# First pair of heads: the second head's loads move to GpSimd, its query cast is split, and one of its transposes moves ahead of the second group

## The chip, the core and the metric

The kernel runs on one core of a Trainium2 chip. The metric is the device time of one execution in microseconds (us). The kernel before took 118.14 us, the median of three runs (117.71, 118.14 and 118.82).

## The reference

Attention over 8 batches and 8 heads of 512 positions and 64 dimensions, in float32, softmax over the keys:

```python
scale = 1.0 / np.sqrt(q.shape[-1])
scores = np.einsum('bhqd,bhkd->bhqk', q, k) * scale
scores = scores - scores.max(axis=-1, keepdims=True)
attn = np.exp(scores)
attn = attn / attn.sum(axis=-1, keepdims=True)
return np.einsum('bhqk,bhkd->bhqd', attn, v).astype(np.float32)
```

## The kernel before

The 64 heads are worked on as 32 pairs. A head has four blocks of 128 queries and four blocks of 128 keys. Q, K and V of a pair are loaded as float32, cast to float16, and Q and K are transposed on TensorE so that the 64 dimensions lie on the partitions. Scores are made transposed: one matmul gives a block of 128 keys on the partitions against all 512 queries, from 64 rows. Two such blocks, one on the upper and one on the lower 64 rows of the array, make a "group", a PSUM tile of 128 x 1024, and one exponential turns it into float16 probabilities in SBUF (line 594; line 780 for the first three groups). Line 683 multiplies the probabilities with V, which carries a column of ones, so that the sums of the softmax come with the result; VectorE inverts and scales (lines 655 and 663), and SyncE stores. Twelve of the groups are exponentiated by VectorE with a polynomial instead (lines 612 and 634), four of these with help from GpSimd (lines 647 and 650). All else of the exponentials is ScalarE's.

The order of the instructions is fixed by hand (`tc.manual_schedule()`). A planner, the class `Plan`, walks through a model of the engines once and gives a list of steps, which are then issued in that order on each engine's queue. It starts behind the first pair of heads with constants, and nothing of it depends on how the first pair is done. Each engine runs its own queue in order, and a wait holds whatever is behind it on that engine.

Ahead of the planner's steps stands the opening, in this order of the source:

- `first_loads` (line 723): Q and K of the first pair, one load of 128 KB for each head. The keys go through ScalarE's queue (line 727), the queries through SyncE's (line 728).
- The loads of the next pairs, 256 KB each, on SyncE's queue (line 498).
- `make_identity`: GpSimd writes `ident`, the identity that every transpose needs. Then VectorE's memsets of `lift` and of the column of ones in V.
- `first_pair` (line 734). Casts to float16: `q16` holds each query block twice side by side, so that a transpose puts it on both the upper and the lower 64 rows. Head 0's casts are spread over VectorE (lines 746, 747), ScalarE (748) and GpSimd (749). Head 1's keys are cast by ScalarE (750), its queries by GpSimd in one instruction (751).
- TensorE, meanwhile, runs `busy` matmuls on a constant (line 732), whose results nobody reads. They are called fillers here. Behind them come head 0's transposes: two blocks of queries, the keys in two pieces, two more blocks of queries, three fillers. VectorE copies the results out of PSUM into `qt` and `kt` (lines 794 to 797).
- The first groups. Group 0 is done in two halves of 256 queries, `st_0a` and `st_0b`, each with an exponential of its own; group 1 is `st1`. Then head 1's four query transposes into `pqb` and two key transposes into `pkb` (lines 808 to 813), VectorE's copies of them (810, 814), four fillers, and group 2, `st2`, with the fourth exponential (line 818). Group 3 is the first of the planner's (line 589), followed by the transposes of pair 1 (line 544) and VectorE's copies of them (line 551).

In this text the scores of `st_0a`, `st_0b`, `st1` and `st2` are called first, second, third and last scores, and the exponentials of line 780 first to fourth.

Of the kernel before, what the change touches and what calls it, by code (L numbers as in the profile page):

```python
# [404 lines left out]
def kernel(  # L405
# [7 lines left out]
    nc = tc.nc  # L413
    B, H, S, D = q.shape
    P = 128
    NI = S // P
# [56 lines left out]
    def source(src, g):  # L473
        b, h = g // ppb, 2 * (g % ppb)
        return src[b, h : h + 2].rearrange("h (p i) d -> p h i d", i=NI)

    def load_tile(g, name):
        t = lpool.tile(
            [P, 2, NI, D],
            FP32,  # L480
            tag=f"{name}32",
            name=f"{name}32_{g}",
            bufs=7,
        )
        raw.setdefault(g, {})[name] = t
        return t
# [75 lines left out]
    def buffer(b, name):  # L562
        return ps_st.tile([P, 2, S], FP32, tag=f"st{b}", name=name)
# [159 lines left out]
    def first_loads():  # L723
        tk = load_tile(0, "k")
        tq = load_tile(0, "q")
        for h in range(2):
            nc.scalar.dma_start(out=tk[:, h], in_=source(k, 0)[:, h])
            nc.sync.dma_start(out=tq[:, h], in_=source(q, 0)[:, h])

    def busy(dst, n):  # L730

        nc.tensor.matmul(dst[:, 0:n], ones[:, 0:P], ones[:, 0:n], start=True, stop=True)  # L732

    def first_pair():


        tk, tq = raw[0]["k"], raw[0]["q"]
        k16 = cpool.tile([P, 2, NI, D], FP16, name="k16_0")
        q16 = cpool.tile([P, 2, NI, 2, D], FP16, name="q16_0")
        kt = cpool.tile([P, 2, 2, P], FP16, name="kt_0")  # L740
        qt = cpool.tile([P, 2, NI, P], FP16, name="qt_0")

        def twice(h, i, n):
            return tq[:, h, i : i + n].rearrange("p i (x d) -> p i x d", x=1).broadcast_to([P, n, 2, D])

        nc.vector.tensor_copy(out=q16[:, 0, 0:2], in_=twice(0, 0, 2))
        nc.vector.tensor_copy(out=k16[:, 0, 0:2], in_=tk[:, 0, 0:2])
        nc.scalar.copy(q16[:, 0, 2:4], twice(0, 2, 2))
        nc.gpsimd.tensor_copy(out=k16[:, 0, 2:4], in_=tk[:, 0, 2:4])
        nc.scalar.copy(k16[:, 1], tk[:, 1])  # L750
        nc.gpsimd.tensor_copy(out=q16[:, 1], in_=twice(1, 0, NI))

        pka, st1, st0 = (buffer(b, f"st_{n}") for b, n in enumerate(("ka", "1", "0a")))
        pqa = ps_x.tile([P, 8, P], FP16, tag="x0", name="tp_qa")
        pqb = ps_x.tile([P, 8, P], FP16, tag="x1", name="tp_qb")

        pka, pkc, pqc = pka[:, 0, :], st1[:, 0, :], st1[:, 1, :]
        pka, pkc, pqc = (
            t.bitcast(FP16).rearrange("p (n c) -> p n c", c=P) for t in (pka, pkc, pqc)
        )  # L760

        def t_k(dst, h, j):
            nc.tensor.transpose(
                dst, k16[:, h, 2 * j : 2 * j + 2, :].rearrange("p i d -> p (i d)"), ident
            )

        def t_q(dst, h, i):
            nc.tensor.transpose(dst, q16[:, h, i].rearrange("p x d -> p (x d)"), ident)

        def first_scores(st, h, j, q0, q1, pt, s0, s1):  # L770
            for x in range(2):
                s = slice(64 * x, 64 * x + 64)
                nc.tensor.matmul(
                    st[:, x, s0:s1],
                    kt[s, h, j, :],
                    qt[s, h].rearrange("p i c -> p (i c)")[:, q0:q1],
                    start=True,
                    stop=True,
                )
            nc.scalar.activation(  # L780
                out=pt[:, :, q0:q1], in_=st[:, :, s0:s1], func=EXP, scale=scale
            )

        for n in range(6):
            busy(st0[:, 0], S)
        for n in range(2):
            busy(st0[:, 0], P)
        for i in range(2):
            t_q(pqa[:, i], 0, i)
        t_k(pka[:, 0], 0, 0)  # L790
        t_k(pkc[:, 0], 0, 1)
        for i in range(2):
            t_q(pqc[:, i], 0, 2 + i)
        nc.vector.tensor_copy(out=qt[:, 0, 0:2], in_=pqa[:, 0:2])
        nc.vector.tensor_copy(out=kt[:, 0, 0], in_=pka[:, 0])
        nc.vector.tensor_copy(out=qt[:, 0, 2:4], in_=pqc[:, 0:2])
        nc.vector.tensor_copy(out=kt[:, 0, 1], in_=pkc[:, 0])
        for n in range(3):
            busy(st0[:, 1], P)
        pts = [ppool.tile([P, 2, S], FP16, tag="pt", name=f"pt_{m}") for m in range(3)]  # L800
        for m in range(3):
            for x, b in enumerate(groups[m]):
                blocks[b] = pts[m][:, x, :]
        first_scores(st0, 0, 0, 0, 256, pts[0], 0, 256)
        st0b = buffer(0, "st_0b")
        first_scores(st0b, 0, 0, 256, 512, pts[0], 0, 256)
        first_scores(st1, 0, 1, 0, S, pts[1], 0, S)
        for i in range(NI):
            t_q(pqb[:, i], 1, i)
        nc.vector.tensor_copy(out=qt[:, 1], in_=pqb[:, 0:4])  # L810
        pkb = ps_x.tile([P, 8, P], FP16, tag="x0", name="tp_kb")
        for j in range(2):
            t_k(pkb[:, j], 1, j)
        nc.vector.tensor_copy(out=kt[:, 1], in_=pkb[:, 0:2])
        st2 = buffer(2, "st_2")
        for n in range(4):
            busy(st2[:, 0], P)
        first_scores(st2, 1, 0, 0, S, pts[2], 0, S)
        first.update(kt=kt, qt=qt)

    with tc.manual_schedule():
        plan = Plan(groups, NP, 3)
        steps = plan.run()
        first_loads()
        for g, name in plan.first_loads:
            load(g, name)
# [5 lines left out]
        for n in range(NV):  # L832
            nc.vector.memset(vps[n][:, :, :, D : D + 1], 1.0)
        first_pair()
        do = {
            "transposes": transposes,
# [46 lines left out]
```

## Time and profile before

| | us |
|---|---|
| median of three runs | 118.14 |
| the profiled execution | 117.7 |
| its span on the core | 115.9 |
| ScalarE busy | 109.1 (94%) |
| TensorE matmuls busy | 105.8 (91%) |
| VectorE busy | 101.6 (88%) |
| GpSimd busy | 78.9 (68%) |
| DMA engines, mean share of the span in queue 1 (SyncE) | 86.5% |

Times in the profile are counted from the start of the span. PE is TensorE, with PEld its loads of weights; DVE is VectorE, ACT ScalarE, POOL GpSimd, SP SyncE. A "q" behind the name of an engine means its queue's own work, such as issuing a DMA. A row of the timeline gives start, duration, engine, line, operation, output and inputs, shape and, in brackets, how long the engine was idle before it and what released it. The duration of a matmul covers its way through the array, so neighbouring matmuls overlap; the pace is read from their starts. In the groups of instructions, the numbers behind the bar are busy time in us and the mean of one in ns, and behind the second bar the idle time before them.

The loads of the opening, read from the trace:

| load | issued | landed |
|---|---|---|
| queries, head 0 (SyncE) | 0.72 | 3.31 |
| keys, head 0 (ScalarE) | 0.71 | 3.48 |
| queries, head 1 (SyncE) | 1.14 | 3.94 |
| keys, head 1 (ScalarE) | 1.15 | 4.19 |
| keys, pair 1 (SyncE) | 1.61 | 5.17 |
| queries, pair 1 (SyncE) | 2.08 | 6.00 |

### The profile page before, as it was taken

What the parts mean: (1) busy time and instruction counts of PE and PEld (TensorE: products, weight loads), DVE (VectorE), ACT (ScalarE), POOL (GpSimd) and SP (SyncE); (2) the same over time, 40 slices, a digit from 0 to 9 for tenths busy, and PEclk for the clock granted to TensorE, in tenths of its full rate; (3) what the DMA queues carried; (4) which work ended last, traced back from release to release, by engine and by line L of the source; (5) the groups of instructions that cost most, each with busy time, mean ns of one, the idle gap of its engine ahead of it and who ended that gap; (6) DMA issues with size and microseconds to landing.
All of it is one profiled execution on the core that took longest, in us unless ns stands there. A gap on an engine that the chain in (4) does not pass through costs nothing.

```text
span 115.9 us, 4106 instructions
## 1 busy us (share of the span) xinstructions
PE 105.8 (91%) x1583; PEld 67.1 (58%) x1583; DVE 101.6 (88%) x180; ACT 109.1 (94%) x121; POOL 78.9 (68%) x122
## 2 busy tenths in 40 slices
PE   7979997999989998899979999999999999899980
PEld 2546563657557565476655565765666665567660
DVE  4463599999999999999999999999999999999381
ACT  4499999999999999999999999999999999999980
POOL 2579870895995799676946999679995598740000
PEclk9999999999999999999999999999999999999999
DMA  3999999999999999999996899999999972035354
GB/s 105 326 373 378 384 380 382 383 376 322 343 367 338 306 362 385 369 378 354 316 296 210 264 320 343 294 312 369 328 306 314 332 269 94 0 96 184 95 187 133
DMA packets 35604, 33.83 MB, mean 292 GB/s; under 512 B 2688, under 2 KB 35584, under 8 KB 35584
## 3 DMA queue, kind: packets, MB, share of 16 engines
q1 hardware_dynamic: 35152, 33.24, 86.5%
q10 hardware_dynamic: 432, 0.33, 0.9%
q8 instruction: 12, 0.20, 0.7%
q14 instruction: 8, 0.07, 0.1%
HBM read 25.17 MB, written 8.39 MB: 289 GB/s over the span
## 4 chain that ended last, share of the span: by engine, by line
ACT 28%; PE 20%; DVE 15%; POOL 12%; issue 12%; DMA 8%; SPq 3%; POOLq 0%; ACTq 0%
ACT pt L594 27%; PE o L683 7%; PE st L589 6%; DMA v<-in_v_dram 5%; POOL qkp L519 5%; DVE ring L663 4%; POOL vp L504 3%; PE st_0a L732 3%; DMA out_dram<-ring 3%; DVE tqk L557 2%; DVE y L634 2%; DVE z L612 2%; DVE pd L634 2%; POOL t L647 2%; POOL k L517 2%
## 5 line engine op out<-in xcount | busy, mean ns | idle before, releaser
L594 ACT ACTIVATE pt<-st 128x1024 f16<-128x1024 f32 (+1 forms) x114 | 104.1, 1075 | 0.1
L589 PE MATMUL st<-tqk 64*128 64x512 f16 (+1 forms) x250 | 46.1, 381 | 4.2 <-ACT pt L594 3.1
L683 PE MATMUL o<-vp,pt 128*128 128x65 f16 x912 | 43.1, 194 | 0.7 <-DVE ring L663 0.6
L683 PEld LDWEIGHTS <-pt 128*128 128x128 f16 x912 | 35.6, 98 | 13.0 <-issue 10.3
L504 POOL CAST vp<-v 128x512 f16<-128x512 f32 x32 | 19.2, 616 | 10.4 <-DVE pd L634 5.9
L519 POOL CAST qkp<-k 128x512 f16<-128x512 f32 x31 | 21.0, 678 | 4.7 <-PE o L683 2.5
L663 DVE TENSOR_TENSOR ring<-o,rc 128x448 f32<-128x448 f32 (+2 forms) x37 | 22.6, 611 | 1.1
L589 PEld LDWEIGHTS <-tqk 64*128 64x128 f16 x250 | 13.2, 93 | 17.4 <-issue 8.7
L557 DVE COPY tqk<-tp 128x1024 f16<-128x1024 f16 x30 | 20.3, 676 | 3.0 <-PE tp L544 3.0
L519 POOL CAST qkp<-q 128x512 f16<-128x512 f32 x30 | 19.4, 646 | 4.4 <-DVE pd L634 4.0
L544 PE MATMUL tp<-ident,qkp 128*128 128x128 f16 x248 | 19.6, 219 | 0.8 <-DVE ring L663 0.5
L544 PEld LDWEIGHTS <-qkp 128*128 128x128 f16 x248 | 14.2, 97 | 8.4 <-issue 3.6
L634 DVE SCALAR_TENSOR_TENSOR pd<-y,z 128x1024 uint32<-128x1024 f32 x12 | 14.9, 1246 | 0.0
L612 DVE TENSOR_SCALAR z<-st 128x1024 f32<-128x1024 f32 x12 | 14.6, 1218 | 0.2 <-PE st L589 0.2
L634 DVE SCALAR_TENSOR_TENSOR y<-st,z 128x1024 f32<-128x1024 uint16 x12 | 14.6, 1215 | 0.0
L683 PE MATMUL o<-vp,pd 128*128 128x65 f16 x96 | 14.5, 194 | 0.0
L683 PEld LDWEIGHTS <-pd 128*128 128x128 f16 x96 | 9.4, 98 | 1.4 <-issue 1.2
L655 DVE RECIPROCAL rc<-o 128x7 f32<-128x7 f32 (+2 forms) x37 | 7.3, 197 | 2.9 <-PE o L683 2.6
L650 POOL TENSOR_TENSOR y<-t,y 128x1024 f32<-128x1024 f32 x4 | 9.5, 2364 | 0.3
L517 POOL TENSOR_SCALAR k<-k 128x128 f32<-128x128 f32 x12 | 6.3, 528 | 1.8 <-DVE pd L634 1.2
L634 DVE SCALAR_TENSOR_TENSOR y<-z,y 128x1024 f32<-128x1024 uint16 x4 | 5.4, 1344 | 0.0
L634 DVE SCALAR_TENSOR_TENSOR y<-st,y 128x1024 f32<-128x1024 uint16 x4 | 4.9, 1216 | 0.0
(53 smaller groups left out, 37.8 us busy)
## 6 DMA issues: line engine op xcount, KB each, us to landing
out_dram<-ring SPq DMA_DIRECT2D x63, 128.0 KB, 3.8
k<-in_k_dram SPq DMA_DIRECT2D x31, 256.0 KB, 5.1
q<-in_q_dram SPq DMA_DIRECT2D x31, 256.0 KB, 5.1
v<-in_v_dram SPq DMA_DIRECT2D x27, 256.0 KB, 4.8
v<-in_v_dram SPq DMA_DIRECT2D x10, 128.0 KB, 3.6
k<-in_k_dram ACTq DMA_DIRECT2D x2, 128.0 KB, 2.9
q<-in_q_dram SPq DMA_DIRECT2D x2, 128.0 KB, 2.7
out_dram<-obl SPq DMA_DIRECT2D x1, 64.0 KB, 1.6
```

The lines of the kernel that those rows point to most:

```text
L504: return nc.gpsimd.tensor_copy(out=vps[g % NV][:, :, :, 0:D], in_=raw[g]["v"][:, :, :, :])
L517: ins = nc.gpsimd.tensor_scalar(out=x, in0=x, scalar1=LOG2E, scalar2=None, op0=AluOp.mult)
L519: ins = nc.gpsimd.tensor_copy(out=dst, in_=src[:, :, :, :])
L544: nc.tensor.transpose(tps[g][:, n, i, :], qkp[g][:, n, i, :], ident)
L557: nc.vector.tensor_copy(out=tqk[g][:, :, :], in_=tps.pop(g).rearrange("p n i c -> p n (i c)"))
L589: nc.tensor.matmul(st[:, x, cols], kc, qc[:, cols], start=not on_dve, stop=True)
L594: nc.scalar.activation(out=pt[:, :, cols], in_=st[:, :, cols], func=EXP, scale=scale)
L612: nc.vector.tensor_scalar(out=r["z"][:, :, :], in0=r["st"][:, :, :], scalar1=128.0, scalar2=2.0**17, op0=AluOp.mult, op1=AluOp.max,)
L634: nc.vector.scalar_tensor_tensor(out=r["bits"][:, :, :] if last else y, in0=(low, one, y)[s], scalar=(QUARTIC if shared else CUBIC)[s], in ...
L650: nc.gpsimd.tensor_tensor(out=y[:, :, :], in0=t[:, :, :], in1=y[:, :, :], op=AluOp.mult)
L663: nc.vector.tensor_tensor(out=ring[:, u % NU : u % NU + n, :], in0=o[:, x : x + n, 0:D], in1=rc[:, 0:n].broadcast_to([P, n, D]), op=AluOp. ...
L683: nc.tensor.matmul(os[u // 7][:, u % 7, :], blocks[(g, c, h)][:, y * P : (y + 1) * P], vps[g % NV][:, h, c, :], start=(c == 0), stop=(c == ...
```

## The change

Five places of the opening change; the planner and its steps are the same.

- Queries and keys of head 1 are loaded through GpSimd's queue, as the first things that GpSimd does, ahead of the identity. SyncE and ScalarE each issue one load less.
- GpSimd casts head 1's queries in two instructions of two blocks each.
- The first run of fillers is six of 512 columns and one of 256, instead of six of 512 and two of 128.
- A filler of 128 columns is put between first and second scores; it writes a part of `st_0b`'s PSUM tile that the scores leave free. The last run of fillers has three instead of four.
- The first of head 1's four query transposes is put between second and third scores. The other three stay behind the third scores.

```diff
     def first_loads():
         tk = load_tile(0, "k")
         tq = load_tile(0, "q")
-        for h in range(2):
-            nc.scalar.dma_start(out=tk[:, h], in_=source(k, 0)[:, h])
-            nc.sync.dma_start(out=tq[:, h], in_=source(q, 0)[:, h])
+        nc.gpsimd.dma_start(out=tq[:, 1], in_=source(q, 0)[:, 1])
+        nc.gpsimd.dma_start(out=tk[:, 1], in_=source(k, 0)[:, 1])
+        nc.scalar.dma_start(out=tk[:, 0], in_=source(k, 0)[:, 0])
+        nc.sync.dma_start(out=tq[:, 0], in_=source(q, 0)[:, 0])
...
         nc.gpsimd.tensor_copy(out=k16[:, 0, 2:4], in_=tk[:, 0, 2:4])
+        nc.gpsimd.tensor_copy(out=q16[:, 1, 0:2], in_=twice(1, 0, 2))
+        nc.gpsimd.tensor_copy(out=q16[:, 1, 2:4], in_=twice(1, 2, 2))
         nc.scalar.copy(k16[:, 1], tk[:, 1])
-        nc.gpsimd.tensor_copy(out=q16[:, 1], in_=twice(1, 0, NI))
...
-        for n in range(6):
-            busy(st0[:, 0], S)
-        for n in range(2):
-            busy(st0[:, 0], P)
+        for n in (512, 512, 512, 512, 512, 512, 256):
+            busy(st0[:, 0], n)
...
         st0b = buffer(0, "st_0b")
+        for n in range(1):
+            busy(st0b[:, 0, 256:512], P)
         first_scores(st0b, 0, 0, 256, 512, pts[0], 0, 256)
+        for i in range(1):
+            t_q(pqb[:, i], 1, i)
         first_scores(st1, 0, 1, 0, S, pts[1], 0, S)
-        for i in range(NI):
+        for i in range(1, NI):
             t_q(pqb[:, i], 1, i)
...
-        for n in range(4):
+        for n in range(3):
             busy(st2[:, 0], P)
         first_scores(st2, 1, 0, 0, S, pts[2], 0, S)
```

## The prediction, made before the changed kernel had run

> **What bounds the kernel now.** I read the groups of instructions first, then ScalarE's timeline over the first 9 us, then the same stretch of TensorE, GpSimd, VectorE and SyncE, and last the waits. The group that carries the time:
>
> ```profile
> L594 ACT ACTIVATE pt<-st 128x1024 f16<-128x1024 f32 (+1 forms) x114 | 104.1, 1075 | 0.1
> ```
>
> ScalarE's 114 exponentials at line 594 are 104.1 us busy, with 0.1 us idle before them. In the trace they start 0.904 us apart wherever nothing disturbs them, 0.92 on the mean. So the end is where this stream starts plus a length that the change does not edit. The profiled execution took 117.7 us, its span is 115.9, so 1.8 lies around it; the median of the runs, 118.14, is 0.44 above it. The change edits only what stands before the stream, which ScalarE's timeline shows (start, duration, instruction, in brackets the idle time before it and its releaser):
>
> ```profile
> 3.33 0.40 ACT L748 CAST q<-q 128x256 f16<-128x256 f32 x1 [0.42 <-DMA q<-in_q_dram]
> 4.21 0.41 ACT L750 CAST k<-k 128x256 f16<-128x256 f32 x1 [0.47 <-DMA k<-in_k_dram]
> 5.19 0.60 ACT L780 ACTIVATE pt<-st_0a 128x512 f16<-128x512 f32 x1 [0.58 <-PE st_0a L773]
> 5.69 0.59 ACT L780 ACTIVATE pt<-st_0b 128x512 f16<-128x512 f32 x1
> 6.17 1.03 ACT L780 ACTIVATE pt<-st 128x1024 f16<-128x1024 f32 x1
> 7.48 1.02 ACT L780 ACTIVATE pt<-st 128x1024 f16<-128x1024 f32 x1 [0.29 <-PE st L773]
> ```
>
> The first exponential waits for TensorE, the second and third only for ScalarE, and the fourth for TensorE again: it could have started 0.92 after the third, at 7.09, and started at 7.48. From there the stream is closed, so the fourth exponential's start is what the change has to move. What leads to it:
>
> ```profile
> 3.68 0.40 PE L768 MATMUL tp_qa<-ident,q 128*128 128x128 f16 x2
> 4.30 0.53 PE L732 MATMUL st_0a<-const-bfloat16-1.0 128*128 128x128 bf16 x3
> 4.76 0.40 PE L773 MATMUL st_0a<-qt,kt 64*128 64x256 f16 x2
> 4.95 0.42 PE L773 MATMUL st_0b<-qt,kt 64*128 64x256 f16 x2
> 5.16 0.64 PE L773 MATMUL st<-qt,kt 64*128 64x512 f16 x2
> 5.73 0.60 PE L768 MATMUL tp_qb<-ident,q 128*128 128x128 f16 x4
> 6.12 0.42 PE L763 MATMUL tp_kb<-ident,k 128*128 128x128 f16 x2
> ...
> 7.05 0.39 PE L773 MATMUL st<-qt,kt 64*128 64x512 f16 x2 [0.19 <-DVE kt L814]
> ...
> 7.59 0.62 PE L544 MATMUL tp<-ident,qkp 128*128 128x128 f16 x8
> ```
>
> Chain: four query transposes (5.73), two of the keys, VectorE's copies (0.42 from 6.37, then 0.28 from 6.71), the scores at 7.05, the fourth exponential 0.43 later. Two readings matter. First, pace: the page's clock row prints full speed throughout, but the starts of neighbouring matmuls are 0.107 us apart for 128 columns and 0.427 for 512 until about 6.6, and 0.056 and 0.213 after it. TensorE runs at half pace through all that is edited. Second, TensorE does not wait between 3.68 and 6.12. The second group's scores could use VectorE's copy from about 4.89 and start at 4.95 because the first pair of matmuls has just passed. And a pair on 64 rows beside work on 128 rows costs a gap: fillers end at 4.51 + 0.107 = 4.62, scores start at 4.76 (0.139); the third pair passes at 5.16 + 0.427 = 5.58, the transposes start at 5.73 (0.137). At full pace these gaps are 0.10.
>
> **The change part by part.** *SyncE and ScalarE issue one load less.* SyncE's issues behind it come about 0.45 earlier (its second issue lasts 0.42), ScalarE's table load likewise. The table load ends at 2.91 and the cast behind it waits for the queries until 3.33: nothing. The earlier loads help casts that GpSimd starts on their landing (5.23, 6.05, 6.72), but pair 1's transposes at 7.59 follow fourth scores directly, so nothing reaches ScalarE. If descriptors of the second head no longer stand behind the first head's on the same queues, the first head might land sooner; the gain ends where the fillers end, at 3.48 instead of 3.68, so it lies between 0 and 0.2. I take 0, as the second head stood behind the first already.
>
> *GpSimd issues two loads ahead of the identity.* No row shows GpSimd issuing one. The nearest is the same instruction on SyncE and ScalarE, 0.37 to 0.47 us; the far end is GpSimd's slowest instruction of the trace, 2.36 us. Queued behind them are memset and select of the identity (0.71 to 1.29, so 0.57), then the cast of the keys. With an issue cost g, the identity is there at 0.71 + 2g + 0.57 + 0.05; the transposes need it at 3.68, so up to g = 1.17 it costs nothing, and above that 2(g - 1.17). The keys' landing: ScalarE's load of the second head landed 2.6 us after its issue ended, hence at 0.71 + 2g + 2.6. ScalarE's cast of them stands ahead of the first exponential, but the later parts below leave ScalarE 0.9 us of room, so this too holds up to g = 1.2. I take the issue row, 0.47, thus 0.
>
> The Trainium skill's page "DMA: Bandwidth & Descriptors", section "Anatomy of one DMA — SWDGE (gpsimd) path", fits a GpSimd load as 2.0 us plus bytes over 436,000 per us; for 131,072 bytes that is an estimate of 2.3 us, and the keys would land in time even if the second issue began a microsecond after the first. No run here shows it.
>
> *Queries' cast in two.* 0.61 becomes twice the 128x256 row on GpSimd (0.40): ending at 4.79 instead of 4.60 if the data lands as now. The moved transpose comes after 5.3, the others after 6.4: nothing. In the built program the moved transpose and the other three have separate waits on GpSimd, so the split does what it says.
>
> *Fillers.* Six of 512 and two of 128 columns become six of 512 and one of 256: the same columns, nothing. Three instead of four before the last scores: they lie under VectorE's copies, nothing.
>
> *A filler between first and second scores.* It works on 128 rows between pairs on 64: 0.137 + 0.107 + 0.139 = 0.383, in a place where TensorE does not wait. Second scores at 5.33, second exponential 5.77 instead of 5.69.
>
> *One transpose between second and third scores.* Again 0.383, so third scores start at 5.16 + 0.766 = 5.92. From start to exponential the first pair took 0.436, of which 0.213 were its columns; with 0.427 that is 0.65, so the third exponential starts at 6.57 (now 6.17).
>
> *What remains.* The three other transposes start at 5.73 + 0.77 = 6.49. The third of them starts between 6.66 (pace doubles at 6.6) and 6.71. VectorE's first copy began 0.26 behind the last transpose at full pace (line 544 to line 551) and 0.35 at half: 6.92 to 7.06. Last scores follow 0.68 later, as from 6.37 to 7.05: 7.60 to 7.74. Fourth exponential 0.43 later: 8.03 to 8.17, instead of 7.48. ScalarE could have taken it at 6.57 + 0.92 = 7.49, so the wait before it grows from 0.29 to about 0.5. Cost 0.55 to 0.69; I take 0.6, as both bounds rest on rows nearby. Were both gaps at the full-pace price, 0.10, it would be about 0.4. Behind it the stream has no idle time to take this up; its spacing above 0.904 adds up to 1.75 us over the span, of which some may be waits that do not move, so down to 0.3 may reach the end.
>
> Sum: 117.7 + 0.6 = 118.3 in the profiled execution, 118.7 as a median.
>
> **The rivals.** *The insertions are free and the start is earlier.* Then the fourth exponential comes at 7.09 and the first head's landing gives its 0.2: 0.6 less, 117.5 as a median. For it: an insertion costs nothing where TensorE waits, and if its pace doubles before 4.7 us it would wait for VectorE's copies (4.89 and 5.02) 0.2 us in all. Against it: at this trace's pace there is no wait, and at full pace two insertions are still 2 x 0.25.
>
> *GpSimd's issues are slow.* From g = 1.17 the identity, and so the whole chain, is late by 2(g - 1.17). For g = 1.6 that is 0.86 more: 119.6; at the far end, 2.36, it is 2.4 more, 121.1. It decides between within 1% and slower from g = 1.46. The same lateness arises if GpSimd cannot work while VectorE does: VectorE's memsets from 0.81 to 2.34 are 1.18 us busy, so g = 0.9 with them on top makes the identity 0.63 late, 119.4. For it: software on an engine that needs 0.2 us for a memset. Against: the nearest row is 0.47.
>
> The Trainium skill speaks against the change here: "SBUF — State Buffer", section "SBUF: two separate sides", says that descriptors of a GpSimd load cannot be written while VectorE runs an operation in a two-port mode. By that rule the memsets need not count, but VectorE's casts from 3.33 on would. No run here shows it.
>
> *TensorE's pace doubles later.* The four new gaps leave TensorE idle for about 0.55 us more between 4.9 and 6.5. If that holds the pace back until about 10, last scores and the next ones cost 0.21 more each, the gap behind them 0.04, and of the 0.41 more for pair 1's eight transposes some 0.3 lies beyond the first of VectorE's two copies (line 551): the scores behind it, and their exponential, come about 0.7 later than forecast, 119.4. For it: TensorE was already filled from 0.76 on and yet ran at half pace until 6.6. Against: it has gaps of 0.14 to 0.2 there now.
>
> The page "TensorE: Matmul & The Clock Gate" of the Trainium skill, Part 1, has the pace decided by windows of 3.4 us that run free of the kernel; by that rule the step at 6.6 falls elsewhere in other runs, and the time of either kernel varies by it.
>
> **How the numbers follow.** Forecast (a few tenths slower) 0.48; free insertions 0.17; slow issues 0.19, of which 0.03 stay within 1%; later pace 0.11, over 1%; a gain over 1%, for which I find no place, 0.05. One per cent, 1.18 us, is about what a measurement of this kernel tells from no change. Within 1%: 0.48 + 0.17 + 0.03 = 0.68; slower 0.16 + 0.11 = 0.27; faster 0.05. The range goes from the free insertions, 117.5, to just above slow issues and later pace, 119.7; only an issue well over 1.6 us lies beyond. The forecast alone would have 118.3 to 119.0.
>
> **What would show it.** In the changed profile: third scores near 5.92, last scores near 7.6, fourth exponential near 8.05 with some 0.5 us idle before it for the scores of line 775, and 0.904 spacing behind it. GpSimd's two issues ending before 2.7, with the select of the identity before 3.6. I am wrong if the fourth exponential starts before 7.5, if the first transposes wait for GpSimd, or if 128 columns still take 0.107 after 7 us.

## The result, and the profile after

| | before | after |
|---|---|---|
| median, 15 runs each (us) | 118.16 (117.61 to 120.87) | 119.06 (118.47 to 121.74) |
| the profiled execution (us) | 117.7 | 119.01 |
| its span (us) | 115.9 | 117.2 |

The changed kernel takes 1.009 times as long, with a 95% interval of 1.0064 to 1.0116: 0.9% slower, on the edge of what was called no change. Some executions run 1.5% or more above the fastest of their kernel: medians and ranges include them, ratios leave them out, and the profiles of two experiments below, the queries alone and the moved cast, are of such executions. The forecast, 118.7 with 117.5 to 119.7, held the time. The trace shows that it did so for another reason than the one forecast.

The group of the page that carries the time (busy time, mean in ns, idle time ahead) has not changed: 104.1 us busy, 0.1 idle.

```profile
L594 ACT ACTIVATE pt<-st 128x1024 f16<-128x1024 f32 (+1 forms) x114 | 104.1, 1081 | 0.1
```

So the time was lost ahead of it, in ScalarE's timeline of the opening. The columns are those of the same view of before: start, duration, instruction, in brackets the idle time and its releaser.

```profile
3.23 0.41 ACT L749 CAST q<-q 128x256 f16<-128x256 f32 x1 [0.80 <-DMA q<-in_q_dram]
6.50 0.41 ACT L753 CAST k<-k 128x256 f16<-128x256 f32 x1 [2.86 <-DMA k<-in_k_dram]
6.81 0.59 ACT L782 ACTIVATE pt<-st_0a 128x512 f16<-128x512 f32 x1
7.30 0.59 ACT L782 ACTIVATE pt<-st_0b 128x512 f16<-128x512 f32 x1
7.78 1.94 ACT L782 ACTIVATE pt<-st 128x1024 f16<-128x1024 f32 x2
```

The first exponential starts at 6.81 instead of 5.19, with no idle time of its own: it stands behind the cast of head 1's keys in ScalarE's order, and that cast waited 2.86 us for the data. All four opening exponentials then run back to back; the fourth, the second of the last row, starts at 8.68 instead of 7.48. The wait ahead of it for TensorE, 0.29 before and forecast at 0.5, is gone. GpSimd's timeline shows the two loads and what stood behind them:

```profile
1.24 0.76 POOL L726 DMA_DIRECT2D q<-in_q_dram  x1 [0.81 <-POOLq L871]
1.99 0.55 POOL L727 DMA_DIRECT2D k<-in_k_dram  x1
2.53 0.22 POOL masks.py:197 MEMSET ident<- 128x128 f16 x1
2.83 0.29 POOL masks.py:199 TENSOR_SCALAR_AFFINE_SELECT ident<-ident 128x128 f16<-128x128 f16 x1
3.42 0.29 POOL L750 CAST k<-k 128x128 f16<-128x128 f32 x1 [0.31 <-DMA k<-in_k_dram]
5.85 0.40 POOL L751 CAST q<-q 128x256 f16<-128x256 f32 x1 [2.14 <-DMA q<-in_q_dram]
```

The issues themselves take 0.76 and 0.55 us and end at 2.54. The identity is there at 3.12, in time for the first transposes at 3.58. But GpSimd's cast of the queries waits for their landing until 5.85. The list of DMA issues of the first 9 us (KB of each, median us from issue to landing) has the reason in one column:

```profile
k<-in_k_dram ACTq DMA_DIRECT2D x1, 128.0 KB, 2.6
q<-in_q_dram SPq DMA_DIRECT2D x1, 128.0 KB, 2.5
q<-in_q_dram POOLq DMA_DIRECT2D x1, 128.0 KB, 4.6
k<-in_k_dram POOLq DMA_DIRECT2D x1, 128.0 KB, 4.5
```

Same bytes, almost twice as long. The landings, to be set beside the table of before:

| load | landed before | landed after |
|---|---|---|
| queries, head 0 | 3.31 | 3.21 |
| keys, head 0 | 3.48 | 3.37 |
| queries, head 1 | 3.94 | 5.80 |
| keys, head 1 | 4.19 | 6.48 |
| keys, pair 1 | 5.17 | 3.93 |
| queries, pair 1 | 6.00 | 7.06 |

Pair 1's keys, needed later, now land 2.5 us ahead of head 1's. TensorE's timeline shows the rest of the change:

```profile
4.71 0.40 PE L775 MATMUL st_0a<-qt,kt 64*128 64x256 f16 x2
5.04 0.29 PE L733 MATMUL st_0b<-const-bfloat16-1.0 128*128 128x128 bf16 x1
5.26 0.39 PE L775 MATMUL st_0b<-qt,kt 64*128 64x256 f16 x2
6.31 0.23 PE L770 MATMUL tp_qb<-ident,q 128*128 128x128 f16 x1 [0.66 <-POOL q L751]
6.47 0.39 PE L775 MATMUL st<-qt,kt 64*128 64x512 f16 x2
7.85 0.39 PE L775 MATMUL st<-qt,kt 64*128 64x512 f16 x2
```

The second scores come 0.55 behind the first (0.19 before), so the filler cost 0.36 there. The moved transpose makes the third scores wait for the late queries, until 6.47. Neither is what ends last here: ScalarE takes the third scores only at 7.78.

### The profile page after: what moved, and what is told of

It is laid out like the page before. It is cut to its first block, busy times and chain, and to the rows that moved or that the text cites. A ratio compares the mean times of both kernels' runs of the same rounds, so it can differ in the third digit from the quotient of the medians.

```text
span 117.2 us, 4106 instructions
## 1 busy us (share of the span) xinstructions
PE 105.9 (90%) x1582; PEld 66.7 (57%) x1582; DVE 101.5 (87%) x180; ACT 108.8 (93%) x121; POOL 79.9 (68%) x125
## 4 chain that ended last, share of the span: by engine, by line
ACT 30%; DVE 16%; issue 13%; POOL 13%; PE 13%; DMA 12%; SPq 1%; POOLq 0%; ACTq 0%
ACT pt L594 28%; DMA k<-in_k_dram 7%; PE o L683 6%; PE st L589 5%; POOL qkp L519 5%; DVE ring L663 4%; DVE y L634 3%; POOL vp L504 3%; DMA out_dram<-ring 3%; ACT pt L782 2%; POOL k L517 2%; DVE pd L634 2%; DMA v<-in_v_dram 2%; DVE tqk L557 2%; DVE z L612 2%
## 5 line engine op out<-in xcount | busy, mean ns | idle before, releaser
L594 ACT ACTIVATE pt<-st 128x1024 f16<-128x1024 f32 (+1 forms) x114 | 104.1, 1081 | 0.1
L519 POOL CAST qkp<-q 128x512 f16<-128x512 f32 x30 | 20.4, 679 | 4.7 <-DMA k<-in_k_dram 4.4
L519 POOL CAST qkp<-k 128x512 f16<-128x512 f32 x31 | 19.9, 643 | 4.0 <-PE o L683 1.3
L634 DVE SCALAR_TENSOR_TENSOR pd<-y,z 128x1024 uint32<-128x1024 f32 x12 | 15.4, 1285 | 0.0
```

The source lines that it names most:

```text
L519: ins = nc.gpsimd.tensor_copy(out=dst, in_=src[:, :, :, :])
L594: nc.scalar.activation(out=pt[:, :, cols], in_=st[:, :, cols], func=EXP, scale=scale)
L634: nc.vector.scalar_tensor_tensor(out=r["bits"][:, :, :] if last else y, in0=(low, one, y)[s], scalar=(QUARTIC if shared else CUBIC)[s], in ...
```

## The experiments

Starts of exponentials are compared with those of the same exponential in the profiled execution of before. Ratios are to the kernel before, run on the same chip in the same job. Profiled executions differ from each other by a few tenths, so a single start is read to about that.

**The loads back on SyncE and ScalarE, all the rest of the change kept.**

```diff
-        nc.gpsimd.dma_start(out=tq[:, 1], in_=source(q, 0)[:, 1])
-        nc.gpsimd.dma_start(out=tk[:, 1], in_=source(k, 0)[:, 1])
-        nc.scalar.dma_start(out=tk[:, 0], in_=source(k, 0)[:, 0])
-        nc.sync.dma_start(out=tq[:, 0], in_=source(q, 0)[:, 0])
+        for h in range(2):
+            nc.scalar.dma_start(out=tk[:, h], in_=source(k, 0)[:, h])
+            nc.sync.dma_start(out=tq[:, h], in_=source(q, 0)[:, h])
```

> The changed kernel with head 1's loads back on SyncE's and ScalarE's queues; the split cast, the filler and the moved transpose stay. Theory L (late landing: the two loads through GpSimd land at 5.80 and 6.48 and ScalarE's cast of the keys holds the first exponential until 6.81): landings near 3.9 and 4.2 again, first exponential near 5.2. If L is all, the fourth exponential is near 7.5 and the time is that of before, 118.2. Theory P (the two insertions on TensorE cost 0.38 us each, as forecast): the fourth exponential is near 8.05, with about 0.5 us idle before it, and the time 0.5 to 0.6 above before.

Measured: 118.04 (10 runs) against 117.98 (19 runs), ratio 1.0007, interval 0.9977 to 1.0037. In ScalarE's timeline the first and fourth exponentials wait for TensorE again, as they did before the change:

```profile
4.78 0.60 ACT L781 ACTIVATE pt<-st_0a 128x512 f16<-128x512 f32 x1 [0.28 <-PE st_0a L774]
...
7.02 1.02 ACT L781 ACTIVATE pt<-st 128x1024 f16<-128x1024 f32 x1 [0.24 <-PE st L774]
```

The loads are all that the change loses. The split cast, the fillers and the moved transpose together cost nothing that this interval can show; the 0.6 us of the forecast would be a ratio of 1.005, outside it.

**The loads through GpSimd alone, in the kernel before.** The edit is that of the change in `first_loads`, and nothing else.

> The kernel before with nothing changed but head 1's two loads, which go through GpSimd. L: landings near 5.8 and 6.5, first exponential near 6.8, fourth near 8.7, time 0.8 to 1.3 us above before, like the changed kernel. P: landings in time, at most 0.1 us above before.

Measured: 118.74, 119.37, 120.70 and 120.91 in four runs, too few for an interval; the profile is of the second. ScalarE's timeline has the same wait as the whole change:

```profile
6.88 0.40 ACT L751 CAST k<-k 128x256 f16<-128x256 f32 x1 [3.18 <-DMA k<-in_k_dram]
7.19 0.59 ACT L781 ACTIVATE pt<-st_0a 128x512 f16<-128x512 f32 x1
```

The keys landed at 6.86, the fourth exponential started at 9.06. So the loads suffice to make it late. That the loads alone are slower still than the whole change is not shown: the two runs that compare, the lower ones, lie on either side of its 119.06.

**Only the queries through GpSimd, the keys back on ScalarE.**

```diff
         nc.gpsimd.dma_start(out=tq[:, 1], in_=source(q, 0)[:, 1])
-        nc.gpsimd.dma_start(out=tk[:, 1], in_=source(k, 0)[:, 1])
         nc.scalar.dma_start(out=tk[:, 0], in_=source(k, 0)[:, 0])
+        nc.scalar.dma_start(out=tk[:, 1], in_=source(k, 0)[:, 1])
```

> The changed kernel with head 1's keys back on ScalarE's queue; the queries alone go through GpSimd. L with the keys as the gate: first exponential near 5.2, the queries land at 5.0 to 5.8, the transposes follow near 6.3, fourth exponential 8.1 to 8.3, time 0.6 to 0.8 above before, below the changed kernel. If it is not the keys but anything on GpSimd that costs, the time stays at the changed kernel's.

Measured: ratio 1.0036, interval 0.9994 to 1.0078, from 10 runs that scatter from 117.79 to 120.5. The first exponential is back at 4.75. The queries landed at 5.86, no earlier than with both loads there, and the moved transpose made TensorE wait for them 1.37 us; the fourth exponential came at 8.63. The interval is too wide to say that the late queries are free. In this profiled execution, of 120.1 us, TensorE also lost its pace, which delays the fourth exponential as well. The windows show it (stretch, length, PE busy, granted clock, DMA share, GB/s):

```profile
5.00:7.00 2.00, 0.63 (x7) 1.00 1.07 360
7.00:9.00 2.00, 1.82 (x13) 0.50 1.08 370
11.00:13.80 2.80, 2.80 (x24) 0.50 1.09 384
13.80:16.00 2.20, 2.20 (x49) 1.00 1.09 383
```

After the stretch in which TensorE was busy 0.63 of 2.00 us, the granted clock stands at 0.50 from 6.98 to 13.81.

**The change, with SyncE's loads of the next pairs held until ScalarE has cast head 1's keys.** It asks whether GpSimd's loads are slow by themselves or only beside others.

```diff
         first_loads()
-        for g, name in plan.first_loads:
-            load(g, name)
         make_identity(nc, ident)
...
         first_pair()
+        for n, (g, name) in enumerate(plan.first_loads):
+            ins = load(g, name)
+            if n == 0:
+                tc.add_manual_dep(ins.ins, first["cast"].ins.name, SYNC, reason="held")
```

> The changed kernel with SyncE's loads of the next pairs held back until ScalarE has cast head 1's keys, so that GpSimd's two loads have the DMA engines to themselves. Theory C (their descriptors are ready by 2.54 and wait behind SyncE's 256 KB loads): they land by about 4.3 and the first exponential starts by 5.3. Theory G (a load through GpSimd takes 4.5 us by itself): they land at 5.8 and 6.5 as in the changed kernel. The time says nothing, as pair 1's data come late: slower than the changed kernel by 1 to 3 us.

Measured: the keys landed at 4.80 instead of 6.48, the queries at 4.45 instead of 5.80. One row of the DMA issues, and two of ScalarE's timeline:

```profile
k<-in_k_dram POOLq DMA_DIRECT2D x1, 128.0 KB, 2.8
```

```profile
4.82 0.41 ACT L754 CAST k<-k 128x256 f16<-128x256 f32 x1 [1.18 <-DMA k<-in_k_dram]
5.13 0.59 ACT L783 ACTIVATE pt<-st_0a 128x512 f16<-128x512 f32 x1
```

From issue to landing the keys took 2.8 instead of 4.5 us. 1.7 us of the delay are thus the company of SyncE's loads, by one execution of each kernel. The landing was 0.5 later than expected, yet early enough: the fourth exponential started at 7.22, ahead of before. The kernel as a whole took 122.87 in its one run, since the held loads are missing later (GpSimd waits 2.79 us for pair 1's keys); that price is the experiment's own.

The Trainium skill's "DMA: Bandwidth & Descriptors", section "Issuing engines are not separate DMA queues", says that loads issued by ScalarE, SyncE and GpSimd run on the same 16 engines and interleave. This run agrees: holding SyncE's loads brings GpSimd's keys in 1.7 us sooner. By the fit on the same page of the Trainium skill, section "Anatomy of one DMA — SWDGE (gpsimd) path", a load of this size takes an estimated 2.3 us; 2.8 and 3.2 were measured with SyncE's loads held, 4.5 and 4.6 beside them, and the measurement decides.

**The change, with ScalarE's cast of the keys moved behind the second exponential.** If the order of ScalarE's work were all that costs, the late landing would be covered.

```diff
-        nc.scalar.copy(k16[:, 1], tk[:, 1])
...
         first_scores(st0b, 0, 0, 256, 512, pts[0], 0, 256)
+        nc.scalar.copy(k16[:, 1], tk[:, 1])
```

> The changed kernel with ScalarE's cast of head 1's keys put behind the second exponential instead of ahead of the first. Theory L with ScalarE's order as the gate: first exponential near 5.15 and second near 5.65 whatever the keys do; then the cast at the keys' landing (6.2 to 6.9) and the third exponential 0.3 behind it, fourth near 7.9 to 8.3 against 8.68, time 0.3 to 0.8 us below the changed kernel. If the data themselves are the gate and not the order: no gain.

Measured: 120.41, the median of four runs, ratio 1.0143, interval 1.0076 to 1.0211. The expected gain did not come. ScalarE's timeline:

```profile
5.12 0.60 ACT L781 ACTIVATE pt<-st_0a 128x512 f16<-128x512 f32 x1 [1.28 <-PE st_0a L774]
...
6.95 0.40 ACT L808 CAST k<-k 128x256 f16<-128x256 f32 x1 [0.75 <-DMA k<-in_k_dram]
...
8.73 1.02 ACT L781 ACTIVATE pt<-st 128x1024 f16<-128x1024 f32 x1 [0.45 <-PE st L774]
```

Two exponentials got ahead, but the fourth needs the keys themselves and started at 8.73, against 8.68 with the change. The two cannot be compared as they stand: here the keys landed at 6.93, 0.45 later. From the start of the keys' cast to the fourth exponential it is 1.78 us here and 2.18 with the change, so the order may save some 0.4 there, an estimate from one trace of each. Nothing of it is seen in the time: TensorE waited 1.20 for the keys, and its granted clock was half from 8.07 to 14.89. What the order is worth without that loss of pace stays open.

**Two insertions in TensorE's order, in the kernel before.** This prices the step on which the forecast rested.

```diff
         st0b = buffer(0, "st_0b")
+        busy(st0b[:, 0, 256:512], P)
         first_scores(st0b, 0, 0, 256, 512, pts[0], 0, 256)
+        busy(st1[:, 0], P)
         first_scores(st1, 0, 1, 0, S, pts[1], 0, S)
```

> The kernel before plus two fillers of 128 columns, one between first and second scores and one between second and third; nothing else. It prices the insertions without the loads. Theory P as forecast: 0.38 us each while TensorE runs at half pace, about 0.25 at full pace with 0.2 of the sum under a wait, so the fourth exponential 0.3 to 0.77 later than with no filler at the same pace, and the time 0.3 to 0.7 us above before. Theory S (the slack in front of the third and fourth exponential and the pace that comes earlier in most runs hide them): within 0.2 us of before.

Measured: 118.39 (12 runs) against 118.12 (23), ratio 1.0011, interval 0.9979 to 1.0044. TensorE's timeline:

```profile
4.73 0.28 PE L773 MATMUL st_0a<-qt,kt 64*128 64x256 f16 x2
...
5.11 0.28 PE L773 MATMUL st_0b<-qt,kt 64*128 64x256 f16 x2
...
5.48 0.39 PE L773 MATMUL st<-qt,kt 64*128 64x512 f16 x2
```

The pairs start 0.38 and 0.37 apart. Its counterpart is the first experiment's kernel (loads on SyncE's and ScalarE's queues) without the two insertions:

```diff
         first_scores(st0b, 0, 0, 256, 512, pts[0], 0, 256)
-        for i in range(1):
-            t_q(pqb[:, i], 1, i)
         first_scores(st1, 0, 1, 0, S, pts[1], 0, S)
```

The filler between first and second scores is left out too, and the four transposes stand together behind the third scores.

> e1_loads_back without its filler and with all four query transposes behind the third scores: the kernel before with only the cast in two and the joined filler. A look for the same opening at another pace: if TensorE's pace doubles before 5 us here, the third scores start near 5.0 and the fourth exponential near 6.8, against 7.02 in e1 (P: inserts cost 0.2 there); with S it starts near 7.0.

Measured once: 119.37. TensorE's timeline:

```profile
4.41 0.28 PE L774 MATMUL st_0a<-qt,kt 64*128 64x256 f16 x2
4.60 0.28 PE L774 MATMUL st_0b<-qt,kt 64*128 64x256 f16 x2
4.74 0.39 PE L774 MATMUL st<-qt,kt 64*128 64x512 f16 x2
```

Here they are 0.19 and 0.14 apart, so two insertions cost 0.42 (0.75 less 0.33) at the full pace that both executions have there. From the first scores to the fourth exponential it is 2.62 us with them and 2.20 without: the same 0.42. The fourth exponential came at 6.61, earlier than expected, and nothing came of it: pair 1's loads landed at 7.27 and 7.95 in this execution, and ScalarE gave the gain back. The granted clock was also half from 10.47 to 13.88, so the time of this one run says nothing on the insertions. ScalarE's timeline:

```profile
9.82 1.02 ACT L594 ACTIVATE pt<-st 128x1024 f16<-128x1024 f32 x1 [1.25 <-PE st L589]
```

**A stream that starts earlier: the last scores in two halves, in the kernel before.** It asks whether the opening of before can be beaten. The fillers ahead of the last scores are gone, VectorE's copy of the queries is split, and the planner's PSUM buffers are turned by one so that both halves have one.

```diff
         st2 = buffer(2, "st_2")
-        for n in range(4):
-            busy(st2[:, 0], P)
-        first_scores(st2, 1, 0, 0, S, pts[2], 0, S)
+        first_scores(st2, 1, 0, 0, 256, pts[2], 0, 256)
+        st2b = buffer(0, "st_2b")
+        first_scores(st2b, 1, 0, 256, 512, pts[2], 0, 256)
```

> The kernel before with its fourth group in two halves of 256 queries, each with an exponential of its own, and VectorE's copy of head 1's queries in two, so that the first half needs fewer copies; the four fillers are gone, and the planner's PSUM buffers are shifted by one. If the wait before the fourth exponential (0.39 us in the profile of before) is what the opening still loses, its first half starts 0.3 us earlier and the time is 0.2 to 0.3 us below before. If what is gained in the opening is lost again near 54 us, as the trace of e1 suggests (fourth exponential 0.46 earlier, end only 0.1), the time is that of before.

Measured: 118.14 against 118.12, ratio 0.9983, interval 0.9947 to 1.0019 (12 runs). The first half of the fourth exponential started at 6.57, straight behind the third. Most of the gain was lost again at once, as pair 1's loads landed at 6.49 and 7.13 in this execution (5.17 and 6.00 in before). Of group 3's exponential, 0.88 ahead of before's (7.52 against 8.40), the next keeps 0.31 (9.00 against 9.31). ScalarE's timeline:

```profile
9.00 1.94 ACT L594 ACTIVATE pt<-st 128x1024 f16<-128x1024 f32 x2 [0.41 <-PE st L589]
```

**The lateness alone, in two doses, in the kernel before.** Idle casts on ScalarE, whose results nobody reads, delay the first exponential; no load, cast or matmul of the opening is touched. Seven in one kernel, four in another:

```diff
         nc.scalar.copy(k16[:, 1], tk[:, 1])
+        spare = cpool.tile([P, 7, NI, D], FP16, name="spare")
+        for n in range(7):
+            nc.scalar.copy(spare[:, n], tk[:, 1])
```

> The kernel before, its loads untouched, with seven idle casts on ScalarE (0.31 us apart) between the cast of head 1's keys and the first exponential: first exponential near 6.7, fourth near 8.55, as late as in the changed kernel but by ScalarE alone. If the late first exponential is the whole of the change's cost: 0.7 to 1.1 us above before, like the changed kernel. If the loads through GpSimd cost by something else too (they push SyncE's load stream back by about a microsecond): clearly less, 0.5 or below.

> The same with four idle casts: first exponential near 5.75, fourth near 7.65. If the stream of exponentials passes every delay on: up to 0.2 above before where TensorE's pace doubles late (fourth exponential at 7.48), 0.6 to 0.9 where it doubles early, so 0.3 to 0.6 in the median. If what the opening gains or loses in front of about 7.4 is evened out near 39 us by the landing of V's loads, as the traces of e1 and e7 show: at most 0.25 above before.

ScalarE's timeline with seven:

```profile
4.56 2.24 ACT L753 CAST spare<-k 128x256 f16<-128x256 f32 x7
6.70 0.59 ACT L783 ACTIVATE pt<-st_0a 128x512 f16<-128x512 f32 x1
```

and with four:

```profile
4.62 1.32 ACT L753 CAST spare<-k 128x256 f16<-128x256 f32 x4
5.85 0.59 ACT L783 ACTIVATE pt<-st_0a 128x512 f16<-128x512 f32 x1
```

| | first exponential | fourth | ratio (95%) |
|---|---|---|---|
| before | 5.19 | 7.48 | |
| four idle casts | 5.85 | 7.72 | 0.9991 (0.9965 to 1.0016) |
| seven idle casts | 6.70 | 8.57 | 1.0094 (1.006 to 1.0128) |
| the change | 6.81 | 8.68 | 1.009 (1.0064 to 1.0116) |

Seven idle casts, 119.07, give the time of the change, 119.06, with every load on the queue that it had before. The first exponential's start accounts for the whole loss. Four casts delay it by 0.66, of which 0.24 reach the fourth exponential, and nothing of that is to be measured: before's profiled execution lay 0.46 under its median, so a shift of this size is within what its executions do by themselves.

**How a shift at the start travels.** From the traces, the start of an exponential minus that of the same one in before's:

| | at the fourth | near 46 us | near 57 us | at the last |
|---|---|---|---|---|
| the change | +1.20 | +1.21 | +1.21 | +1.12 |
| seven idle casts | +1.09 | +1.36 | +1.20 | +1.09 |
| four idle casts | +0.23 | +0.20 | +0.20 | +0.23 |
| loads back (first experiment) | -0.46 | -0.46 | -0.01 | -0.11 |
| two insertions | -0.13 | -0.13 | +0.39 | +0.27 |

In these profiled executions delays arrive whole, though for the four casts the median does not show it. A start that is earlier is kept on ScalarE until 52 us and is gone at 55, where it waits for TensorE (ScalarE's timeline of the first experiment):

```profile
55.26 1.02 ACT L594 ACTIVATE pt<-st 128x1024 f16<-128x1024 f32 x1 [0.23 <-PE st L589]
```

What leads there goes back, as far as this trace shows it, to 39 us in GpSimd's timeline:

```profile
37.78 0.62 POOL L504 CAST vp<-v 128x512 f16<-128x512 f32 x1 [1.14 <-DVE pd L634]
39.25 0.62 POOL L504 CAST vp<-v 128x512 f16<-128x512 f32 x1 [0.85 <-DMA v<-in_v_dram]
```

and the same two casts in before:

```profile
38.24 0.62 POOL L504 CAST vp<-v 128x512 f16<-128x512 f32 x1 [1.14 <-DVE pd L634]
39.01 0.62 POOL L504 CAST vp<-v 128x512 f16<-128x512 f32 x1 [0.16 <-DVE ring L663]
```

The first of them is 0.46 earlier, the second waits for V's load and is 0.24 later. That load did not come earlier with the rest: it landed at 39.12, against 38.60 in before. GpSimd stays 0.24 behind until 48 us, and its cast at 51.28 is no earlier than before's (51.25). VectorE's step of line 634, started 0.32 earlier at 51.44 beside that cast, takes 1.53 us instead of 1.22 and ends when before's does; TensorE then waits 0.17 for VectorE at 54.40. In the kernel with two insertions V landed at 39.52, the same cast started at 39.64, and the exponentials near 57 us are 0.39 late. So the landing of this load varies by 0.9 between the three, and what an opening gains can be lost to it; that it is so in most executions is not shown.

## Why the prediction was right or wrong

The time was right; the way to it was mostly wrong.

**What bounds the kernel: right.** The stream has 0.1 us idle before and after, and its start decides: +1.20 at the fourth exponential, +1.12 at the last. The median moved by 0.90, the profiled executions by 1.31; before's lay 0.46 under its median, the changed one 0.05 under its own.

**The failed step is the keys' landing.** The prediction put it so: "ScalarE's load of the second head landed 2.6 us after its issue ended, hence at 0.71 + 2g + 2.6", and "I take the issue row, 0.47, thus 0". That gives 4.25; it was 6.48. Of the 2.2 us, 0.9 lie in the issue: it began at 1.24, not 0.71, and took 0.76 and 0.55, so it ended at 2.54 instead of 1.65. The other 1.3 lie behind it: 3.94 us from the end of the issue instead of 2.6. Held apart from SyncE's loads, it was 2.27 (issue end to landing), which is no slower than the row that I had taken. The row was thus not wrong for a load alone; it came from a load with the second place in its queue, and was applied to one that starts later, beside SyncE's loads of 256 KB. The company is not all of it: with only the queries through GpSimd, ScalarE's load of the keys landed 2.82 us after its issue ended (1.60 to 4.42) and GpSimd's of the queries 3.88 after (1.98 to 5.86), beside the same loads of SyncE. Why GpSimd's come off worse there stays open. The prediction had even noted that earlier SyncE issues would follow from the change, and asked only whom they help.

**The room on ScalarE was put too high, and was overrun.** "The later parts below leave ScalarE 0.9 us of room" rests on a fourth exponential at 8.05. With the loads back it came at 7.02, and ScalarE could have started it 0.92 after the third, at 6.67: 0.35 of room. The short dose agrees with the 0.39 that before has: of 0.66 of lateness, 0.24 reached the fourth exponential. With the change the first exponential was 1.6 late (6.81 instead of 5.19).

**The insertions: size right, effect wrong.** Forecast at 0.383 each, or 0.25 at full pace; the filler measured 0.36 in the changed kernel, and two of them 0.42 at full pace. The sentence "From there the stream is closed, so the fourth exponential's start is what the change has to move" failed for small shifts: by the first experiment the insertions cost nothing at the end (1.0007), and its trace loses an earlier start again before 55 us. So the term of 0.6, the whole of the forecast, is nothing, and a term taken as 0 is about 1.1 in the profile. That the two nearly agree is chance.

**The rival of slow issues** named the right engine and the wrong wait. It had the identity late from g = 1.17; g was 0.76 and 0.55, and the identity was ready in time. The wait that came, ScalarE's cast of the keys ahead of the first exponential, was in the part on the loads, as one that holds up to g = 1.2. The rival's second form, VectorE's memsets holding GpSimd, was not tried by itself. The rule from the Trainium skill's "SBUF — State Buffer", section "SBUF: two separate sides", that VectorE's two-port work holds up the writing of descriptors, is not needed for the loss that the held loads remove: in that run VectorE was 1.27 us busy between 3 and 5, and the keys came at 4.80.

**The rival of free insertions** was right that they are free in the end, but not for its reasons: there is no gain of 0.6, and the opening does get 0.42 longer by them at full pace.

**The rival of a later pace** did not happen in the profiled execution: the granted pace doubled at 5.54. Over the profiles it doubled between 3.4 and 6.8. That TensorE can lose its pace by waiting is real: in four profiles it fell back to half (last section). What that costs by itself was not tried.

**Costed at nothing, and nothing:** the cast in two and the fillers, by the first experiment; head 0's landing gained 0.1 (inside the 0 to 0.2). One load less on SyncE, also costed at nothing, brings pair 1's keys forward (issued at 1.17 instead of 1.61) and was not tried apart from the loads through GpSimd.

**The signs that it named.** GpSimd's issues ended before 2.7, the identity came before 3.6, and the first transposes did not wait for GpSimd, all as forecast. The third scores came at 6.47 instead of 5.92, the last at 7.85 instead of 7.6, and the fourth exponential at 8.68 with no idle time instead of 8.05 with 0.5.

## What to carry to other kernels

A load that moves to an idle engine's queue is not a load that lands earlier: price it by its landing beside the other transfers in flight, not by its issue or by a load alone, and then ask which engine has its consumer queued ahead of the bounding stream. Where a stream is closed against delays, it need not be open to gains, since another stream, here the loads, may take over as soon as the first gets ahead. A suspected delay can be dosed by itself, as the idle casts did, and the dose that gives the change's time says whether it is the whole cause.

## What was not expected of the hardware

GpSimd's two loads went out in 64 data packets of 4,096 bytes, which took 0.159 us in the median and up to 0.93, where SyncE's and ScalarE's have 1,024 bytes and 0.046 us in the median; whether it is the packets' size that makes these loads come off worse in company was not tried. Landings scatter even of unchanged loads: pair 1's keys, issued at 1.61 and 1.63, landed at 5.17 in before and at 7.27 in the run without insertions.

TensorE's pace doubled anywhere from 3.4 to 6.8 us. In four executions it fell back to half: from 6.98 to 13.81 (only the queries through GpSimd), from 8.07 to 14.89 (the moved cast), from 11.42 to 18.24 (SyncE's loads held) and from 10.47 to 13.88 (no insertions). In all twelve traces every later change of the granted clock lies a whole multiple of 3.41 us behind the first. Ahead of each of the four falls TensorE was busy 2.04, 2.01, 1.65 and 1.69 of the last 3.41 us, so it was never idle for a whole such stretch; 2.09 of 3.41 was followed by no fall in two others (the loads alone from 5.83, seven idle casts from 6.75). The Trainium skill's "TensorE: Matmul & The Clock Gate", Part 1, has windows of 3.4 us that run free of the kernel; the scatter of the first step and stretches of 3.41 and 6.82 agree.
